# Nine pairs of inner tiles as block products in each feed-forward half of a two-layer decoder trunk

## The chip, the cores and the metric

The kernel runs on one core of a Trainium2 chip. The core has a matrix engine (PE, with its weight loads as PEld), three engines for elementwise work (DVE, ACT and POOL, which is GpSimd) and a queue engine (SP) that mostly issues transfers. The metric is device time in microseconds for the whole program, lower is better. The median of three runs before the change is 2664.32 us (2662.54 to 2666.8).

## The reference

Two layers. Each one is a feed-forward half, a mixer (four kinds of attention with gates), and a second feed-forward half, all on a residual x of 512 tokens by 1024 channels in float32. Only the feed-forward halves change:

```python
def swiglu(h, w_i, w_o):
    gate, up = jnp.split(h @ w_i, 2, axis=-1)
    return (jax.nn.silu(gate) * up) @ w_o

for l in range(DEPTH):                                     # DEPTH = 2
    x = x + 0.5 * swiglu(rms_norm(x, ffn1_norm[l]), ffn1_w_in[l], ffn1_w_out[l])
    ...                                                    # the mixer
    x = x + 0.5 * swiglu(rms_norm(x, ffn2_norm[l]), ffn2_w_in[l], ffn2_w_out[l])
```

`w_i` is 1024 x 5632 and `w_o` is 2816 x 1024, so the inner width of 2816 is 22 tiles of 128.

## The kernel before

All activations stand transposed: channels on the 128 partitions, 512 tokens along the free axis. A product in float32 is made of three matmuls in the type float32r: weight and activation are each split into a high and a low part, and high x high, high x low and low x high are summed (`mm3`, lines 247 to 252). A split is a copy on ACT (high) and a subtraction on DVE (low): `load_split` (line 146) for weights from memory, `split_up` (line 268) for what is already on the core.

A feed-forward half (`ffn`) has two parts. In the inner half, each of the 22 inner tiles takes 16 chained steps over the 8 channel tiles, for gate and for up (`hidden_tile`), 48 matmuls of 512 columns. In the output half, the loop over q takes the 8 output tiles in 4 output pairs (`Pair`), and each sums over the 22 inner tiles.

The inner tiles are of two kinds. The first `nplain = 22 - 2 * npair` are plain: each gives one product of 128 x 128 weights by 512 tokens for each of the two outputs. The others come in pairs, and a pair of inner tiles with a pair of outputs and two halves of 256 tokens makes a 2 x 2 block product in 7 products in place of 8 (Strassen's scheme in Winograd's form). The products have the names a, s, t, b, u, v and d; s, t, u and v use sums of weight tiles: s1 = c + d, s2 = s1 + a, s3 = a + c, s4 = s2 + b. The activation sides (r0 to r3 in `combined`) are made once per half, split, and kept in `fph` and `fpl`, 7 x 256 columns each per pair. Before the change there are 8 pairs, so 6 plain tiles.

`Pair.run` (line 281) does the plain tiles (`whole`), then the pairs in groups of up to four (`group`, line 306). A group loads four weight tiles a, c, d and b, one after another, each with up to 512 columns, one 128 for each pair of the group. Then each of the seven products is split and multiplied over all pairs of the group, so one product of a group of four is 12 matmuls of 256 columns. The buffers matter here: `hi` and `lo`, where splits land, have 4 each and are used in turn by the products in the order a, s, t, b, u, v, d; `raw`, for a and c, has 3; `wb` and `wd`, for b and d, have 1 each; the sums `ws` have 2. A buffer is written again when its last reader is done. The tile d is read first (s1) and last (product d) in its group.

When a product has its last pair, `after` (line 368) folds it into the residual tiles in `y` and `up`, and after v and d the finished tile is stored and the next norm takes its square and its split (`Norm.add`). The square of a tile goes to a tile of the tag `sq`.

The order of the instructions on each engine is made by the framework's planner when the program is built; weight loads, sums and splits of a group have a raised priority (`tc.high_priority`). Each engine then runs its own queue in that order and waits on semaphores. SP issues the weight loads, POOL the residual loads and stores, with descriptors in a ring whose size is `RING`.

Of the kernel before, what the change touches and what calls it, by code (L numbers as in the profile page):

```python
# [12 lines left out]
F32 = mybir.dt.float32  # L13
# [7 lines left out]
P = 128  # L21
# [24 lines left out]
AH = 4  # L46
CW = 512
COL = 64
NPAIRS = (8, 8)
OP_BUFS = dict(x=2, ws=2)  # L50
INTO = dict(b=(0, 0), v=(0, 1), d=(1, 0))
PAD = 24
TH = S // 2
SLOT = dict(a=0, s=5, t=4, b=2, u=1, v=3, d=6)
RING = 8192
OFF = dict(aq=0, ak=512, av=1024, bq=1536, bk=1920, bv=2304, cq=2688, ck=3072, cv=3456,
           dq=3846, dk=4230, dv=4614, gl=4998)
BR_ROW = (0, 512, 896, 1280)
# [41 lines left out]
def trunk_kernel(ctx: ExitStack, tc: tile.TileContext, a, out):  # L100
# [34 lines left out]
    def mm_tile(name):  # L135
        return psm.tile([P, S], F32, tag="mm", name=name)
# [127 lines left out]
    def chain(*args):  # L264
        for _ in chain_steps(*args):
            pass

    def split_up(h, lo, src):
        A.activation(h, src, AF.Copy)
        V.tensor_tensor(lo, src, h.bitcast(F32), ALU.subtract)  # L270

    class Pair:
# [8 lines left out]
        def run(self, out, late=False):  # L281
            self.out = out
            self.x = [self.tile("x", f"x{self.nm}{n}") for n in range(2)]
            for x, src in zip(self.x, self.xs):
                nc.gpsimd.dma_start(x, src)
            n = len(self.paired)
            groups = [(p0, min(4, n - p0)) for p0 in range(0, n, 4)]
            if late:
                assert len(groups) == 1
                self.group(*groups[0], "astu")  # L290
                self.whole()
                self.group(*groups[0], "bvd")
            else:
                self.whole()
                for g in groups:
                    self.group(*g, "astbuvd")
# [95 lines left out]
    def combined(r0, r1, r2, r3):  # L392


        lo, hi = slice(0, TH), slice(TH, S)
        V.tensor_tensor(r2[:, lo], r0[:, lo], r0[:, hi], ALU.subtract)
        V.tensor_tensor(r2[:, hi], r1[:, hi], r2[:, lo], ALU.add)
        V.tensor_tensor(r3, r1[:, lo], r2[:, hi], ALU.subtract)
        V.tensor_tensor(r0[:, hi], r0[:, hi], r1[:, hi], ALU.subtract)


    def ffn(l, w_in, w_out, x_of, nrm, nxt, name, keep, early=None):
        npair = NPAIRS[early is None]
        nplain = NH - 2 * npair
        plain, paired = [], []

        def hidden_tile(j, ip):
            pg = mm_tile(f"pg{name}{j}")
            chain(pg, w_in[l, j, 0], nrm.xh, nrm.xl, f"g{name}{j}")
            pu = mm_tile(f"pu{name}{j}")  # L410
            chain(pu, w_in[l, j, 1], nrm.xh, nrm.xl, f"u{name}{j}")
            g = ip.tile([P, S], F32, tag="g", name=f"g{name}{j}")
            u = ip.tile([P, S], F32, tag="u", name=f"u{name}{j}", bufs=3)
            V.tensor_tensor(g, pg, nrm.rb, ALU.mult)
            A.activation(g, g, AF.Silu)
            V.tensor_tensor(u, pu, nrm.rb, ALU.mult)
            V.tensor_tensor(u, u, g, ALU.mult)
            return u

        with ExitStack() as st:  # L420
            fp = st.enter_context(tc.tile_pool(name=f"ff{name}", bufs=1, reuse_waits="tile"))
            with tc.tile_pool(name=f"fi{name}", bufs=2, reuse_waits="tile") as ip:
                for j in range(nplain):
                    if j == 2 and early is not None:
                        early()
                    u = hidden_tile(j, ip)
                    h = fp.tile([P, S], F32R, tag="fh", name=f"fh{name}{j}", bufs=nplain)
                    lo = fp.tile([P, S], F32R, tag="fl", name=f"fl{name}{j}", bufs=nplain)
                    split_up(h, lo, u)
                    plain.append((h, lo))  # L430
            fq = st.enter_context(tc.tile_pool(name=f"fq{name}", bufs=1, reuse_waits="tile"))
            with tc.tile_pool(name=f"fj{name}", bufs=2, reuse_waits="tile") as ip:
                for p in range(npair):
                    j = nplain + 2 * p
                    r0, r1 = hidden_tile(j, ip), hidden_tile(j + 1, ip)
                    r2 = ip.tile([P, S], F32, tag="r", name=f"r{name}{p}")
                    r3 = ip.tile([P, TH], F32, tag="rs", name=f"rs{name}{p}")
                    combined(r0, r1, r2, r3)
                    h = fq.tile([P, 7 * TH], F32R, tag="fph", name=f"fph{name}{p}", bufs=npair)
                    lw = fq.tile([P, 7 * TH], F32R, tag="fpl", name=f"fpl{name}{p}", bufs=npair)  # L440
                    for n, r in enumerate((r0, r1, r2, r3)):
                        c = slice(n * S, n * S + (S if n < 3 else TH))
                        split_up(h[:, c], lw[:, c], r)
                    paired.append((lambda sl, h=h: h[:, sl], lambda sl, lw=lw: lw[:, sl]))
            nrm.close()
            if nxt is not None:
                nxt.open()
            op = st.enter_context(tc.tile_pool(name=f"fo{name}", bufs=1, reuse_waits="tile"))

            def tile_of(tag, nm):  # L450
                return op.tile([P, TH if tag == "up" else S], F32, tag=tag, name=nm, bufs=OP_BUFS.get(tag, 1))

            for q in range(NK // 2):
                def done(n, x):
                    m = 2 * q + n
                    (nc.sync if nxt is None and m == NK - 1 else nc.gpsimd).dma_start(keep[m], x)
                    if nxt is not None:
                        nxt.add(m, x, lambda nm: tile_of("sq", nm))

                ms = (2 * q, 2 * q + 1)  # L460
                Pair(f"{name}{q}", [w_out[l, m] for m in ms], plain, paired, 0.5, [x_of[m] for m in ms],
                     tile_of).run(done)
# [818 lines left out]
    def kept(name):  # L1281
        return [drm.tile([P, S], F32, name=f"{name}{m}") for m in range(NK)]
# [5 lines left out]
    with tc.tile_pool(name="first", bufs=2) as fp:  # L1288
        x = {}
# [14 lines left out]
    x = [a["x"][m] for m in range(NK)]  # L1304
    for l in range(L):
        xs = kept(f"xs{l}")
        nxt = Norm(l, "nm", f"m_{l}")
        ffn(l, a["f1_in"], a["f1_out"], x, nrm, nxt, f"a{l}", xs, setup_bias if l == 0 else None)
        nxt.finish_cols()
        nrm, nxt = nxt, Norm(l, "n2", f"f2_{l}")  # L1310
        x = kept(f"xt{l}")
        with tc.tile_pool(name=f"acc{l}", bufs=1, reuse_waits="tile") as ap:
            acc = []
            mixer(l, nrm, nxt, xs, x, ap, acc)
        nxt.finish()
        nrm = nxt
        last = l == L - 1
        nxt = None if last else Norm(l + 1, "n1", f"f1_{l + 1}")
        keep = out if last else kept(f"xu{l}")
        ffn(l, a["f2_in"], a["f2_out"], x, nrm, nxt, f"b{l}", keep)  # L1320
        x = keep
        if not last:
            nxt.finish()
            nrm = nxt


def _tiles(w):
    l, k, n = w.shape
    return w.reshape(l, k // P, P, n // P, P).transpose(0, 3, 2, 1, 4).reshape(l, n // P, P, k)


def _out_order(npair):
    first = NH - 2 * npair
    order = list(range(first))
    for p0 in range(0, npair, 4):
        for odd in range(2):
            order += [first + 2 * p + odd for p in range(p0, min(p0 + 4, npair))]
    return order


def _layout(i):
    i = {k: np.asarray(v) for k, v in i.items()}
    r = {"x": i["x"][0].T.reshape(NK, P, S)}
    for n, s in (("f1", "ffn1"), ("f2", "ffn2")):
        t = _tiles(i[s + "_w_in"])
        r[n + "_in"] = np.stack([t[:, :NH], t[:, NH:]], 2)
        t = _tiles(i[s + "_w_out"]).reshape(L, NK, P, NH, P)
        t = np.stack([t[l][:, :, _out_order(NPAIRS[l + (n == "f2") > 0])] for l in range(L)])
        r[n + "_out"] = t.reshape(L, NK, P, HID)
# [42 lines left out]
```

## Time and profile before

| | before |
|---|---|
| median of three runs | 2664.32 us (2662.54 to 2666.8) |
| the profiled execution, its own time | 2664.03 us |
| its span | 2662.2 us |
| PE busy | 2644.1 us, 99% of the span |
| DVE busy | 1735.8 us, 65% |
| ACT busy | 1402.4 us, 53% |
| POOL busy | 349.7 us, 13% |

The span runs from the first to the last instruction of the profiled execution. A matmul's row shows a duration longer than the distance to the next one's start, because matmuls overlap in the engine; so the pace of PE is read from its starts. Names of tiles in the profile leave numbers out: `poa` is `po` of a first feed-forward half (`a`) and `pob` of a second one (`b`). A row such as `hida<-wda` is the high split of product d in a first half, `paa`, `psa` and `pta` are the sums that products a, s and t write.

### The profile page before, as it was taken

Reading aid. Unit: us, or ns where it says so; the run is one execution under the profiler, and the core shown is the slowest. Engines: PE = TensorE matmul, PEld = TensorE weight load, DVE = VectorE, ACT = ScalarE, POOL = GpSimd, SP = SyncE. Lnnn points to the kernel's source line nnn. Section 1 sums busy time; section 2 is a strip of 40 time slices with the busy share of each in tenths; the row PEclk is TensorE's granted clock in tenths of the full one; section 3 lists DMA queues with packets and bytes.
Section 4 is the critical chain, followed back from the end, with each engine's and each line's share of the span. In section 5 each row is a group of like instructions: output and inputs, shape, how many; then the busy total and the mean of one; then the engine's idle time right before and its main releaser. Section 6 shows DMA issues by size and latency. Waiting matters only on the chain.

```text
span 2662.2 us, 40085 instructions
## 1 busy us (share of the span) xinstructions
PE 2644.1 (99%) x14206; PEld 2309.7 (87%) x14206; DVE 1735.8 (65%) x3540; ACT 1402.4 (53%) x2916; POOL 349.7 (13%) x494
## 2 busy tenths in 40 slices
PE   9999999999999999999999999999999999999999
PEld 7888999888988878888988889998889888888898
DVE  5556768777764564557755568587777646645566
ACT  4333458787665643334443334577776556433333
POOL 1000022222222210000000000222222221100000
PEclk9999999999999999999999999999999999999999
DMA  5323442222322343334432334322223223423243
GB/s 167 103 96 103 133 134 73 74 72 89 89 75 80 95 151 101 97 97 122 135 107 95 99 102 141 121 67 79 77 83 94 71 84 100 154 95 97 97 121 118
DMA packets 150985, 272.00 MB, mean 102 GB/s; under 512 B 17977, under 2 KB 48697, under 8 KB 150784
## 3 DMA queue, kind: packets, MB, share of 16 engines
q1 hardware_dynamic: 138960, 233.16, 28.5%
q0 software_dynamic: 10672, 34.19, 4.1%
q8 instruction: 111, 1.82, 0.3%
q10 hardware_dynamic: 1152, 2.10, 0.2%
q14 instruction: 90, 0.74, 0.1%
HBM read 256.70 MB, written 14.90 MB: 102 GB/s over the span
## 4 chain that ended last, share of the span: by engine, by line
PE 96%; DVE 1%; ACT 1%; issue 1%; DMA 1%; POOL 0%; ACTq 0%; POOLq 0%
PE pgl L250 4%; PE pgl L252 4%; PE pgl L251 4%; PE pua L251 3%; PE pua L250 3%; PE pub L252 3%; PE pua L252 3%; PE pub L251 3%; PE pub L250 3%; PE pga L251 3%; PE pga L252 3%; PE pga L250 3%; PE pgb L252 3%; PE pgb L251 3%; PE pgb L250 3%; PE pob L251 2%
## 5 line engine op out<-in xcount | busy, mean ns | idle before, releaser
L250 PE MATMUL pgl<-xhm,higl 128*128 128x512 f32 x512 | 215.7, 421 | 0.0
L252 PE MATMUL pgl<-xhm,logl 128*128 128x512 f32 x512 | 201.0, 393 | 0.0
L251 PE MATMUL pgl<-xlm,higl 128*128 128x512 f32 x512 | 200.5, 392 | 0.0
L250 PE MATMUL pga<-xhf,higa 128*128 128x512 f32 x352 | 137.4, 390 | 2.1 <-ACT xhf L204 2.1
L251 PE MATMUL pga<-xlf,higa 128*128 128x512 f32 x352 | 137.4, 391 | 0.7 <-DVE xlf L205 0.7
L252 PE MATMUL pga<-xhf,loga 128*128 128x512 f32 x352 | 137.7, 391 | 0.0
L250 PE MATMUL pgb<-xhf,higb 128*128 128x512 f32 x352 | 137.7, 391 | 0.0
L252 PE MATMUL pua<-xhf,loua 128*128 128x512 f32 x352 | 137.3, 390 | 0.0
L251 PE MATMUL pua<-xlf,hiua 128*128 128x512 f32 x352 | 137.3, 390 | 0.0
L250 PE MATMUL pua<-xhf,hiua 128*128 128x512 f32 x352 | 137.2, 390 | 0.0
L251 PE MATMUL pub<-xlf,hiub 128*128 128x512 f32 x352 | 136.9, 389 | 0.0
L252 PE MATMUL pub<-xhf,loub 128*128 128x512 f32 x352 | 136.9, 389 | 0.0
L251 PE MATMUL pgb<-xlf,higb 128*128 128x512 f32 x352 | 136.9, 389 | 0.0
L250 PE MATMUL pub<-xhf,hiub 128*128 128x512 f32 x352 | 136.9, 389 | 0.0
L252 PE MATMUL pgb<-xhf,logb 128*128 128x512 f32 x352 | 136.9, 389 | 0.0
L152 ACT ACTIVATE hiua<-rawua 128x512 fp32r<-128x512 f32 x88 | 55.7, 633 | 135.7 <-PE pua L251 119.5
L152 ACT ACTIVATE hiub<-rawub 128x512 fp32r<-128x512 f32 x88 | 55.6, 633 | 131.1 <-PE pub L251 130.4
L155 POOL TENSOR_TENSOR logl<-rawgl,higl 128x512 fp32r<-128x512 f32 x64 | 84.0, 1313 | 249.9 <-ACT higl L152 215.2
L252 PEld LDWEIGHTS pgl<-xhm,logl 128*128 128x128 f32 x512 | 96.1, 188 | 21.9
L155 DVE TENSOR_TENSOR loua<-rawua,hiua 128x512 fp32r<-128x512 f32 x88 | 60.4, 687 | 78.8 <-ACT hiua L152 78.8
L250 PEld LDWEIGHTS pgl<-xhm,higl 128*128 128x128 f32 x512 | 96.6, 189 | 15.8
L251 PEld LDWEIGHTS pgl<-xlm,higl 128*128 128x128 f32 x512 | 96.9, 189 | 13.1
(823 smaller groups left out, 8452.0 us busy)
## 6 DMA issues: line engine op xcount, KB each, us to landing
rawgl<-in_w_gate SPq DMA_DIRECT2D x128, 256.0 KB, 2.6
rawga<-in_f_in SPq DMA_DIRECT2D x88, 256.0 KB, 2.5
rawua<-in_f_in SPq DMA_DIRECT2D x88, 256.0 KB, 2.6
rawgb<-in_f_in SPq DMA_DIRECT2D x88, 256.0 KB, 2.5
rawub<-in_f_in SPq DMA_DIRECT2D x88, 256.0 KB, 2.6
rawmo<-in_w_out SPq DMA_DIRECT2D x32, 256.0 KB, 2.7
rawt0a<-in_w_tok_a SPq DMA_DIRECT2D x32, 192.0 KB, 2.4
rawbqk<-in_w_bqk SPq DMA_DIRECT2D x24, 256.0 KB, 2.6
```

The lines of the kernel that those rows point to most:

```text
L152: A.activation(hi[:, :n], raw[:, :n], AF.Copy)
L155: eng.tensor_tensor(lo[:, :n], raw[:, :n], hi[:, :n].bitcast(F32), ALU.subtract)
L250: T.matmul(ps, wh, xh, start=first, stop=False)
L251: T.matmul(ps, wh, xl, start=False, stop=False)
L252: T.matmul(ps, wl, xh, start=False, stop=last)
```

## The change

Nine pairs in place of eight in each feed-forward half, so 18 inner tiles go through block products and 4 stay plain. The groups have up to three pairs in place of four: three groups of three, with weight tiles of 384 columns and 9 matmuls to a product. The plain tiles of an output are then one weight load of 512 columns in place of two of 512 and 256. Three more edits take memory away: the quarter-size tile `rs` has one buffer in place of two, the squares are written to the tag `y` in place of one of their own, and the descriptor ring is 4096 bytes in place of 8192. `_out_order` lays the weights out on the host in the order in which the groups load them.

```diff
--- before.py
+++ after.py
@@ -46,13 +46,14 @@
 AH = 4
 CW = 512
 COL = 64
-NPAIRS = (8, 8)
+NPAIRS = (9, 9)
+GRP = 3
 OP_BUFS = dict(x=2, ws=2)
 INTO = dict(b=(0, 0), v=(0, 1), d=(1, 0))
 PAD = 24
 TH = S // 2
 SLOT = dict(a=0, s=5, t=4, b=2, u=1, v=3, d=6)
-RING = 8192
+RING = 4096
 OFF = dict(aq=0, ak=512, av=1024, bq=1536, bk=1920, bv=2304, cq=2688, ck=3072, cv=3456,
            dq=3846, dk=4230, dv=4614, gl=4998)
 BR_ROW = (0, 512, 896, 1280)
@@ -284,7 +285,7 @@
             for x, src in zip(self.x, self.xs):
                 nc.gpsimd.dma_start(x, src)
             n = len(self.paired)
-            groups = [(p0, min(4, n - p0)) for p0 in range(0, n, 4)]
+            groups = [(p0, min(GRP, n - p0)) for p0 in range(0, n, GRP)]
             if late:
                 assert len(groups) == 1
                 self.group(*groups[0], "astu")
@@ -434,7 +435,7 @@
                     j = nplain + 2 * p
                     r0, r1 = hidden_tile(j, ip), hidden_tile(j + 1, ip)
                     r2 = ip.tile([P, S], F32, tag="r", name=f"r{name}{p}")
-                    r3 = ip.tile([P, TH], F32, tag="rs", name=f"rs{name}{p}")
+                    r3 = ip.tile([P, TH], F32, tag="rs", name=f"rs{name}{p}", bufs=1)
                     combined(r0, r1, r2, r3)
                     h = fq.tile([P, 7 * TH], F32R, tag="fph", name=f"fph{name}{p}", bufs=npair)
                     lw = fq.tile([P, 7 * TH], F32R, tag="fpl", name=f"fpl{name}{p}", bufs=npair)
@@ -455,7 +456,7 @@
                     m = 2 * q + n
                     (nc.sync if nxt is None and m == NK - 1 else nc.gpsimd).dma_start(keep[m], x)
                     if nxt is not None:
-                        nxt.add(m, x, lambda nm: tile_of("sq", nm))
+                        nxt.add(m, x, lambda nm: tile_of("y", nm))
 
                 ms = (2 * q, 2 * q + 1)
                 Pair(f"{name}{q}", [w_out[l, m] for m in ms], plain, paired, 0.5, [x_of[m] for m in ms],
@@ -1332,9 +1333,9 @@
 def _out_order(npair):
     first = NH - 2 * npair
     order = list(range(first))
-    for p0 in range(0, npair, 4):
+    for p0 in range(0, npair, GRP):
         for odd in range(2):
-            order += [first + 2 * p + odd for p in range(p0, min(p0 + 4, npair))]
+            order += [first + 2 * p + odd for p in range(p0, min(p0 + GRP, npair))]
     return order
```

## Rows read from the trace of the kernel before

**Rows 1.** engine table of the page: busy us, share of the span, instructions

```profile
PE 2644.1 (99%) x14206; PEld 2309.7 (87%) x14206; DVE 1735.8 (65%) x3540; ACT 1402.4 (53%) x2916; POOL 349.7 (13%) x494
```

**Rows 2.** windows view, two groups: PE, PEld, DVE, ACT, POOL busy (instructions), PEclk, DMA, GB/s

```profile
291.00:311.20 20.20, 20.20 (x169) 20.16 (x169) 14.96 (x27) 8.57 (x15) 0.00 (x0) 1.00 0.39 111
```

**Rows 3.** groups by line: engine, tiles, shape, xcount | busy, mean ns | idle before

```profile
L250 PE MATMUL poa<-fha,hioa 128*128 128x512 f32 x96 | 37.4, 390 | 0.0
...
L250 PE MATMUL paa<-fpha,hiaa 128*128 128x256 f32 x64 | 18.1, 282 | 0.0
```

**Rows 4.** timeline of PE: start us, duration us, engine, line, instruction

```profile
254.36 0.39 PE L250 MATMUL poa<-fha,hioa 128*128 128x512 f32 x1
...
262.52 0.28 PE L250 MATMUL paa<-fpha,hiaa 128*128 128x256 f32 x1
...
295.37 0.28 PE L250 MATMUL poa<-fpha,hiba 128*128 128x256 f32 x1
...
302.57 0.28 PE L250 MATMUL psa<-fpha,hisa 128*128 128x256 f32 x1
```

**Rows 5.** timeline of ACT, DVE and SP at one seam, [idle before <-releaser]

```profile
295.50 0.63 ACT L269 ACTIVATE hida<-wda 128x512 fp32r<-128x512 f32 x1 [0.57 <-PE pta L251]
...
296.17 0.69 DVE L270 TENSOR_TENSOR loda<-wda,hida 128x512 fp32r<-128x512 f32 x1 [0.51 <-ACT hida L269]
...
296.89 0.33 SPq L317 DMA_DIRECT2D wda<-in_f_out  x1
...
299.79 0.69 DVE L323 TENSOR_TENSOR s1a<-wca,wda 128x512 f32<-128x512 f32 x1 [1.49 <-DMA wda<-in_f_out]
300.51 0.69 DVE L323 TENSOR_TENSOR s2a<-s1a,waa 128x512 f32<-128x512 f32 x1
...
301.32 0.63 ACT L269 ACTIVATE hisa<-s2a 128x512 fp32r<-128x512 f32 x1 [3.75 <-PE poa L252]
```

**Rows 6.** tile view of wda, then timelines of ACT and PE at three places

```profile
DMA to landing us min/median/max: 2.8/3.0/4.2
...
1681.07 0.63 ACT L269 ACTIVATE hisa<-s2a 128x512 fp32r<-128x512 f32 x1 [5.07 <-PE paa L251]
1681.61 0.62 ACT L269 ACTIVATE hita<-s1a 128x512 fp32r<-128x512 f32 x1
...
1680.88 0.28 PE L252 MATMUL paa<-fpha,loaa 128*128 128x256 f32 x1
1681.76 0.39 PE L250 MATMUL psa<-fpha,hisa 128*128 128x256 f32 x1 [0.60 <-ACT hisa L269]
...
1682.50 0.28 PE L251 MATMUL pta<-fpla,hita 128*128 128x256 f32 x1
...
274.15 0.28 PE L251 MATMUL psa<-fpla,hisa 128*128 128x256 f32 x1
...
274.61 0.28 PE L251 MATMUL pta<-fpla,hita 128*128 128x256 f32 x1
```

**Rows 7.** passes over 384 columns (source, groups), page's DMA issues (KB, us to landing)

```profile
L155 DVE TENSOR_TENSOR lot1a<-rawt1a,hit1a x16: 545/558/1005, 1688.6 to 1759.8; 128x384 fp32r<-128x384 f32 x16
...
L152 ACT ACTIVATE hit1a<-rawt1a 128x384 fp32r<-128x384 f32 x32 | 16.7, 526 | 16.1 <-PE pt1a L544 6.8 <-DMA rawt1a<-in_w_tok_a 4.9 <-issue 1.6
...
rawgl<-in_w_gate SPq DMA_DIRECT2D x128, 256.0 KB, 2.6
...
rawt0a<-in_w_tok_a SPq DMA_DIRECT2D x32, 192.0 KB, 2.4
```

**Rows 8.** timeline of DVE and ACT at the start of the first output half

```profile
260.19 0.69 DVE L323 TENSOR_TENSOR s1a<-wca,wda 128x512 f32<-128x512 f32 x1
...
261.72 0.64 ACT L269 ACTIVATE hisa<-s2a 128x512 fp32r<-128x512 f32 x1 [2.99 <-DVE s2a L323]
```

**Rows 9.** timeline of POOL: DMA issues of the bias table and of its first use

```profile
51.35 0.52 POOL L512 DMA_DIRECT2D scr<-flat  x1 [0.97 <-DMA scr<-flat]
...
373.34 2.15 POOL L529 DMA_DIRECT2D bias0A<-scr  x4
```

## The prediction

> **What bounds the kernel now.** I read the engine table first: PE is busy in 99% of the span [rows 1]. A busy PE need not run at its peak, so the windows view of one stretch of the feed-forward output half comes next. There PE is busy for all of 20.2 us at the full granted clock (1.00, 2.4 GHz), and DVE for 14.96 us, 74% [rows 2]. What the reader is to see there is a PE-bound stage with one engine close behind. The timeline then gives the pitch, the distance between two starts. The 36 matmuls of 512 columns between 254.36 and 262.52 come 0.2267 us apart, the 60 of 256 columns between 295.37 and 302.57 come 0.1200 us apart [rows 4]. The counts by line say how many there are: 96 high-times-high plain matmuls of one layer name are 2 layers x 4 output pairs x 2 outputs x 6 inner tiles, 64 of one block product are 2 x 4 x 8 pairs [rows 3]. So an output pair costs 36 x 0.2267 + 168 x 0.1200 = 28.3 us, and there are 16 of them (4 halves x 4). Last I followed one seam, where group 0 of an output pair ends and group 1 begins, instruction by instruction over four engines [rows 5]. It decides the forecast.
>
> **The matmuls.** For each output pair, two plain inner tiles go: 2 tiles x 2 outputs x 3 = 12 matmuls of 512 columns, 12 x 0.2267 = 2.72 us. One more pair comes: 7 products x 3 = 21 matmuls of 256 columns, 21 x 0.1200 = 2.52 us. The gain is 0.20 us, times 16: 3.2 us. The inner half runs the same matmuls.
>
> The Trainium skill (TensorE: Matmul & The Clock Gate, Back-to-back issue gap) gives a pitch of N/2.4 + 2.5 ns: 215.8 and 109.2 ns, so an estimate of 16 x (2.59 - 2.29) = 4.8 us. The trace does not agree, 226.7 and 120.0 ns [rows 4], and the measurement decides.
>
> **The seam, and why groups of three pairs hurt it.** The sum of weights `s` needs the tile `wd` of its own group (s1 = c + d, s2 = s1 + a), and `wd` has one buffer. So the load of the next `wd` waits until product d of the group before has split its own, and that split waits for a `hi` buffer, which product t releases (four buffers, d comes four after t). From there a chain runs beside PE [rows 5]: hida starts 295.50, loda 296.17, the load is issued 296.89, s1 starts 299.79, s2 300.51, hisa 301.32 and ends 301.95: 6.45 us. PE meanwhile works through b, u, v, d and the next a, 5 x 12 matmuls, and reaches s at 302.57 [rows 4], 7.07 us after hida's start. So the slack is only 0.6 us.
>
> After the change each product has 9 matmuls. PE's cover shrinks by 5 x 3 x 0.1200 = 1.80 us, to 5.27 us. The chain shrinks less. A pass over 384 columns takes 0.558 us on DVE and 0.526 us on ACT [rows 7], against the 0.69 and 0.63 of 512 [rows 5]: -0.13 and -0.10. I take a load of 192 KB as 0.2 us shorter: the page's issue table has 2.4 us for 192 KB and 2.6 for 256 KB [rows 7]. Link by link: 0.57 + 0.59 + 2.70 + 0.59 + 0.68 + 0.53 = 5.66, and 0.06 from hisa's end to the matmul (1681.07 + 0.63 to 1681.76) [rows 6] makes 5.72. So s is 0.45 us late at each seam. There were 16 seams inside output pairs (2 groups each); with 3 groups there are 32. 32 x 0.45 = 14.4 us. The queue of ACT makes it worse: hita stands behind hisa, 0.54 us after it [rows 6], so after two matmuls of s PE may wait some 0.2 us again. I keep that for the range, because PE's order may fill it.
>
> What this looks like can already be seen where a load came late. The load of `wd` takes 3.0 us at the median and 4.2 once; at the seam behind that one PE's starts from 1680.88 to 1682.50 take 1.62 us for 4 steps worth 0.48: 1.14 us lost, with hisa as releaser [rows 6]. One seam per half, the first, also loses 0.22 us (274.15 to 274.61, 2 steps) [rows 6]. 1.14 + 4 x 0.22 = 2.0 us is all that the 16 seams lose now; I take it off, since the 14.4 count every seam anew.
>
> Bounds per seam: below 0, if PE has another product ready. Above: no shorter load (+0.20), the 0.2 behind hita, and t finishing two matmuls later, as it does in groups whose t is interleaved with b (+0.24): 1.1 us, or 35 us in all. I take 0.45, from the row with the usual load.
>
> The Trainium skill (DMA: Bandwidth & Descriptors, Anatomy of one DMA) puts a DMA at about 2.0 us fixed plus bytes/436e3: 2.45 us for 192 KB, 2.60 for 256 KB, so three quarters of the bytes save 0.15 us, which speaks against smaller groups. The trace agrees roughly, 2.4 and 2.6 [rows 7]; by the rule the sum would be 32 x 0.05 = 1.6 us higher.
>
> **The entry of the output half.** PE starts the plain tiles at 254.36 and reaches the first s 12 matmuls of product a after 262.52, at 263.96 [rows 4]. With 24 plain matmuls and 9 of product a it gets there at 254.36 + 5.44 + 1.08 = 260.88. DVE is then still splitting the last pair: s1 starts at 260.19 and hisa ends at 262.35 [rows 8]. With the shorter passes this is 260.06 + 0.59 + 0.68 + 0.53 = 261.86, plus 0.06: 1.04 us late, where there was a slack of 1.55. Four halves: 4.2 us. The bounds are 0 (the last pair's splits can stand behind s1) and 1.4 each. I take 1.04. From one output pair to the next the plain tiles cover: 5.44 + 1.08 us lie between the last d and s, more than the 5.27.
>
> **What costs nothing.** DVE gets 33 passes in place of 22 in an output pair's groups: 11 x 0.558 = 6.1 us of a group's 63 x 0.12 = 7.56, 81%, still under PE; if that cover went, the upper bound above holds it. The small tile of `combined` with one buffer is read within the pair and written again only after two hidden tiles, 96 matmuls or 21.8 us later. The squares wait in `y` for each other and for z: one pass of ACT and one of DVE, 0.63 + 0.69 [rows 5], hidden behind the next plain tiles; at the end of three halves they could show, 3 x 1.3 = 4 us at most, taken as 0. The descriptor ring: GpSimd waits in one place for its own transfers, 0.97 us for the bias table at 51.35, and that table is not read before 373.34 [rows 9]. If half as many fitted, it would wait there for a landing or two more, hidden by over 300 us. In the output half GpSimd has two loads and two stores per 28 us. So 0.
>
> **Sum.** On the profiled execution, 2664.03 us (a span of 2662.2 and 1.8 around it; the median of the three runs is 2664.32, so no correction): 2664.03 - 3.2 + 14.4 + 4.2 - 2.0 = 2677.4 us, 0.5% slower.
>
> **Rivals.**
> - *PE's order covers the seam.* If b or t is split and multiplied ahead of s (t needs only s1, 0.59 us sooner than s2; b needs neither), 0.45 us of lateness is hidden. For it: PE already takes two matmuls of t between those of s [rows 6], and `wb` comes earlier than `wd`. Against: ACT does hisa, then hita, then hiba at each seam that I followed, though hita's operand is ready first, and a later t makes the next d later. Then only the matmuls count: 2664.03 - 3.2 = 2660.8, not slower; down to 2658.8 if the 2.0 us of present stalls go too. It decides from 0.1 us of lateness per seam downwards (32 x 0.1 = the gain of 3.2).
> - *The seam at its upper bound.* Loads as slow as before and t interleaved everywhere: 32 x 1.1 = 35, so 2664.0 - 3.2 + 35 + 4.2 - 2.0 = 2698 us. For it: the load at 1675.31. Against: of the two halves of a pair's groups only one interleaves.
> - *The faster pitch.* Were PE to take 109.2 and 215.8 ns, as the first page's rule says, and the seams covered, it would be 2664.0 - 4.8 - 2.0 = 2657.2. Rows 4 speak against it.
>
> **How the numbers follow.** Forecast 0.50, covered seam 0.34, upper bound 0.09, faster pitch 0.02, and 0.05 for something unseen (0.04 of it no change). 0.2% is 5.3 us, about what a measurement of this kernel tells from no change. The forecast's own range is 2668 to 2692 (0.2 to 0.9 us per seam, entry included), all slower. The covered case lies within 0.2% but for its lowest end, 0.04 of its 0.34. So faster 0.04 + 0.02 + 0.01 = 0.07, same 0.30 + 0.04 = 0.34, slower 0.50 + 0.09 = 0.59. A range from 2659 to 2694 leaves out half of the upper case and the lowest end of the covered one.
>
> **What would show it.** Right: at both seams of an output pair PE's first psa matmul starts 0.3 to 0.7 us after the last paa at pitch, with hisa as releaser, and the chain hida to hisa takes 5.6 to 5.9 us; 12 plain and 21 product matmuls per pair at the same pitches; output halves of 113 + 4 us. Wrong: products b or t ahead of s at the seams and PE at its pitch, output halves near 112.5 us; or a waiting GpSimd.

## The result, and the profile after

The changed kernel takes 2721.18 us (median of 4 runs, 2718.38 to 2723.84), beside 2664.25 us for the kernel before in the same session (4 runs). The ratio is 1.0213, 95% interval 1.0201 to 1.0225: 57 us slower, where 13 were forecast, and above the forecast's range of 2668 to 2692. The profiled span is 2719.8 us, 57.6 more than before.

First the engine table and the chain of waits of the page after (share of the span by engine along the chain that ended last), then the same chain of the page before.

```profile
PE 2665.8 (98%) x14350; PEld 2328.8 (86%) x14350; DVE 1771.4 (65%) x3708; ACT 1419.3 (52%) x3006; POOL 350.7 (13%) x494
...
PE 89%; DVE 4%; DMA 4%; ACT 2%; issue 1%; ACTq 0%; POOL 0%; DVEq 0%; SPq 0%; POOLq 0%
...
PE 96%; DVE 1%; ACT 1%; issue 1%; DMA 1%; POOL 0%; ACTq 0%; POOLq 0%
```

PE still shows 98% of the span [rows 1], so the engine table says almost nothing. The chain says more: before, PE held 96% of it, now 89%, and DMA and DVE have 4% each. The groups by line say that the matmuls are the forecast ones: 64 plain and 72 of one block product, against 96 and 64 [rows 3].

```profile
L251 PE MATMUL poa<-fha,hioa 128*128 128x512 f32 x64 | 25.1, 392 | 0.0
L251 PE MATMUL paa<-fpha,hiaa 128*128 128x256 f32 x72 | 20.3, 282 | 0.0
```

The waits view names the place (who waits, <- for whom: us in total, times, longest). Three rows of after stand first, then one of before.

```profile
DVE s1a L324 <- DMA wda<-in_f_out: 36.2, 18, 4.0
DVE s1b L324 <- DMA wdb<-in_f_out: 34.2, 18, 3.4
PEld psa L251 <- ACT hisa L270: 22.7, 17, 3.1
...
DVE s1a L323 <- DMA wda<-in_f_out: 13.9, 8, 2.8
```

Before, s1 waited 13.9 and 12.1 us for `wd`, 8 times each. Now it waits 36 and 34 us, 18 times each, and PE waits behind it for the split of s, 33 times in all. To size this I took every distance between two starts of PE in the four output halves, less the pitch of its shape [rows 4], and summed what is left. That is 2.4 us before and 60.7 us after. With 3.2 us of matmuls saved, the halves account for 60.7 - 2.4 - 3.2 = 55.1 of the 57.6 us.

The 60.7 us fall into three kinds of place. In all of them s is late: the first matmul of product s starts later than one pitch after the matmul ahead of it, and that excess is the lateness given here. A seam is the step from one group of an output pair to the next, the entry is the first group of an output half.

**The second seam of a pair (group 1 to 2).** A timeline of ACT, DVE, SP and PE at one of them answers to [rows 5]:

```profile
305.01 0.52 ACT L270 ACTIVATE hiva<-wba 128x384 fp32r<-128x384 f32 x1 [1.34 <-DVE wba L324]
305.44 0.51 ACT L270 ACTIVATE hida<-wda 128x384 fp32r<-128x384 f32 x1
...
304.06 0.28 PE L251 MATMUL poa<-fpha,hiba 128*128 128x256 f32 x1
...
305.02 0.28 PE L253 MATMUL pta<-fpha,lota 128*128 128x256 f32 x1
...
306.62 0.33 SPq L318 DMA_DIRECT2D wda<-in_f_out  x1
...
309.11 0.56 DVE L324 TENSOR_TENSOR s1a<-wca,wda 128x384 f32<-128x384 f32 x1 [1.65 <-DMA wda<-in_f_out]
...
310.37 0.52 ACT L270 ACTIVATE hisa<-s2a 128x384 fp32r<-128x384 f32 x1 [3.50 <-DVE s2a L324]
310.80 0.51 ACT L270 ACTIVATE hita<-s1a 128x384 fp32r<-128x384 f32 x1
...
310.18 0.28 PE L253 MATMUL paa<-fpha,loaa 128*128 128x256 f32 x1
310.95 0.38 PE L251 MATMUL psa<-fpha,hisa 128*128 128x256 f32 x1 [0.49 <-ACT hisa L270]
```

From hida's start to the first matmul of s the chain takes 5.51 us, and PE would have reached s at 310.30, 5.28 us after t's last matmul. The chain itself is 0.21 us shorter than forecast (the load takes 2.49 us to s1, not 2.70). But hida starts 0.42 us behind t's last matmul, since it stands behind hiva on ACT, and hiva waits for DVE. 0.42 + 5.51 - 5.28 = 0.65 us late. After two matmuls of s PE loses another 0.28 us in all, as hita stands behind hisa. So 0.93 us at this seam, near the upper bound of 1.1; the median of the fourteen late ones among the sixteen is the same.

The forecast's 0.45 us can be followed to these 0.65. Two matmuls of b now run ahead of t's last one (304.06 and the next), which takes 0.24 us of cover. Hida stands 0.42 us behind t's last matmul, where at the seam of [rows 5] it stood 0.25 behind it (PE, before):

```profile
295.25 0.28 PE L252 MATMUL pta<-fpha,lota 128*128 128x256 f32 x1
```

So 0.45 + 0.24 + 0.17 - 0.21 = 0.65.

**The first seam of a pair (group 0 to 1).** In the first output pair of a half it is like the second or better. In the twelve later ones s is 0.70 to 3.04 us late, 19.7 us together. The worst of them, in a timeline of POOL, SP, DVE and PE:

```profile
1677.52 0.54 POOL L286 DMA_DIRECT2D xa<-xu  x1 [3.45 <-DVE wba L324]
...
1679.17 0.34 SPq L318 DMA_DIRECT2D wda<-in_f_out  x1
...
1683.96 0.56 DVE L324 TENSOR_TENSOR s1a<-wca,wda 128x384 f32<-128x384 f32 x1 [4.03 <-DMA wda<-in_f_out]
...
1682.64 0.28 PE L253 MATMUL paa<-fpha,loaa 128*128 128x256 f32 x1
1685.80 0.58 PE L251 MATMUL psa<-fpha,hisa 128*128 128x256 f32 x1 [2.88 <-ACT hisa L270]
1686.18 0.42 PE L252 MATMUL psa<-fpla,hisa 128*128 128x256 f32 x1
1686.39 0.41 PE L251 MATMUL pta<-fpha,hita 128*128 128x256 f32 x1
```

From the issue of the load to s1 it is 4.79 us here, not 2.49. GpSimd had issued the load of a residual tile 1.65 us earlier. In all twelve such a load is issued 0.5 to 2.3 us ahead of `wd`'s, and there `wd`'s load takes 3.42 us to s1 on the mean (2.73 to 4.79).

What PE does next is seen in the windows view (PE, PEld, DVE, ACT, POOL busy, PEclk, DMA, GB/s):

```profile
1685.80:1691.70 5.90, 5.90 (x27) 5.90 (x28) 3.53 (x7) 2.23 (x5) 0.00 (x0) 0.50 0.43 114
1691.70:1697.00 5.30, 5.30 (x46) 5.30 (x45) 3.36 (x7) 2.30 (x6) 0.00 (x0) 0.97 0.21 46
```

Behind 3.16 us from one start to the next the granted clock is 0.50, the 1.2 GHz level, for 5.9 us. The 256-column matmuls start about 0.21 us apart instead of 0.12. Six such stretches lie in the four output halves, three behind an entry and three behind a seam. They cost 9.6 us beyond the pitch and the 0.28, 2.5 of them in the stretch shown. [Rows 2] of before show 1.00, and its halves have no such stretch.

**The entry.** A row of SP's waits, then a timeline of DVE, SP and PE at the first one; they answer to [rows 8]. The last row is SP's load of `wd` there before:

```profile
SPq L318 <- DVE fpla L271: 17.0, 2, 8.5
```

```profile
257.82 0.68 DVE L271 TENSOR_TENSOR fpla<-ua,fpha 128x512 fp32r<-128x512 f32 x1
...
258.52 0.33 SPq L318 DMA_DIRECT2D wda<-in_f_out  x1
...
260.95 0.56 DVE L324 TENSOR_TENSOR s1a<-wca,wda 128x384 f32<-128x384 f32 x1 [2.11 <-DMA wda<-in_f_out]
...
260.34 0.28 PE L253 MATMUL paa<-fpha,loaa 128*128 128x256 f32 x1
262.79 0.39 PE L251 MATMUL psa<-fpha,hisa 128*128 128x256 f32 x1 [2.17 <-ACT hisa L270]
...
255.99 0.43 SPq L317 DMA_DIRECT2D wda<-in_f_out  x1
```

The first load of `wd` waits up to 8.5 us for a split of the last hidden pair: at the first entry it is issued 0.02 us after DVE has read that pair's tile `u` for the last time (257.82 + 0.68). Before, it was issued at 255.99, ahead of those splits. So s is 2.33 us late here, 9.5 us over the four halves.

In sum: late s at entries 9.5, late s at seams 31.1, the 0.28 us behind each late s 9.2, half clock 9.6, others 1.3.

### The profile page after: what moved, and what is told of

The parts are those of the page before. It is cut to its first block, busy times and chain, and to the rows that moved or that the text cites. A ratio compares the mean times of both kernels' runs of the same rounds, so it can differ in the third digit from the quotient of the medians.

```text
span 2719.8 us, 40867 instructions
## 1 busy us (share of the span) xinstructions
PE 2665.8 (98%) x14350; PEld 2328.8 (86%) x14350; DVE 1771.4 (65%) x3708; ACT 1419.3 (52%) x3006; POOL 350.7 (13%) x494
## 4 chain that ended last, share of the span: by engine, by line
PE 89%; DVE 4%; DMA 4%; ACT 2%; issue 1%; ACTq 0%; POOL 0%; DVEq 0%; SPq 0%; POOLq 0%
PE pgl L251 4%; PE pgl L253 4%; PE pgl L252 4%; PE pua L252 3%; PE pua L251 3%; PE pub L251 3%; PE pub L252 3%; PE pub L253 3%; PE pua L253 3%; PE pga L252 3%; PE pga L253 3%; PE pgb L253 3%; PE pgb L251 3%; PE pgb L252 3%; PE pga L251 3%; DMA wda<-in_f_out 2%
## 5 line engine op out<-in xcount | busy, mean ns | idle before, releaser
L153 ACT ACTIVATE higa<-rawga 128x512 fp32r<-128x512 f32 x88 | 55.5, 632 | 103.4 <-PE pga L252 80.6
```

Source lines behind the costliest of these rows:

```text
L153: A.activation(hi[:, :n], raw[:, :n], AF.Copy)
```

## The experiments

My theory A was: `wd`'s one buffer makes s late at both seams, traffic of the residual tiles makes the first seam worse, the entry waits through shared memory, and the clock falls after the long waits. The rivals were the memory edits (M), and smaller groups or the ninth pair as such (B, N), with their added passes and transfers. All times stand beside runs of the kernel before on the same chip, whose medians were 2664.15 to 2664.83 us. "Gaps" is the sum of PE's start distances over the pitch in the four output halves.

| run | time, us | ratio to before, 95% interval | gaps, us |
|---|---|---|---|
| before | 2664.25 | 1 | 2.4 |
| after | 2721.18 | 1.0213 [1.0201, 1.0225] | 60.7 |
| d_early | 2680.56 | 1.0056 [1.0040, 1.0073] | 15.6 |
| wd2 | 2682.98 | 1.0069 [1.0054, 1.0084] | 17.7 |
| mem_only | 2661.56 | 0.9987 [0.9978, 0.9997] | 2.9 |
| grp3 | 2694.59 | 1.0110 [1.0094, 1.0125] | 27.0 |
| no_resid | 2710.10 | 1.0172 [1.0156, 1.0187] | 48.5 |
| entry | 2706.84 | 1.0164 [1.0150, 1.0178] | 45.4 |
| both | 2667.28 | 1.0011 [1.0002, 1.0020] | 2.1 |
| mix | 2658.81 | 0.9980 [0.9971, 0.9989] | 1.6 |
| exit | 2658.62 | 0.9977 [0.9968, 0.9986] | 2.0 |
| mem_d8 | 2659.88 | 0.9981 [0.9973, 0.9990] | 0.4 |

**d_early: product d right behind t, in groups that are not the last.**

```diff
-                    self.group(*g, "astbuvd")
+                    self.group(*g, "astbuvd" if g is groups[-1] else "astdbuv")
```

> The changed kernel with one edit: in the two groups of an output pair that are not its last, product d is run right behind t instead of last, so that the one buffer of wd is free about 60 matmuls earlier. Theory A (the loop through wd's one buffer, d's split -> load -> s1 -> s2 -> split of s, makes s late at both seams of a pair, and the waits pull the clock down): the 31 us of late s at seams and the 9 us of gaps just behind it go, s stays late at the four entries (9.5 us and some of the half-clock time): 2675 us, 2668 to 2684. Rival B (smaller groups cost by themselves: more splits and more passes on ScalarE and VectorE): nothing moves, 2716 to 2724. Rival C (only a part of the loss hangs on wd; the loads are slow because of the x traffic whatever the order): 2690 to 2705.

Measured 2680.56 us, 40.6 less than after, by one change of order. At the same seam as above, timeline of SP and DVE, then the waits view:

```profile
301.20 0.33 SPq L318 DMA_DIRECT2D wda<-in_f_out  x1
...
303.68 0.56 DVE L324 TENSOR_TENSOR s1a<-wca,wda 128x384 f32<-128x384 f32 x1 [0.17 <-DMA wda<-in_f_out]
```

```profile
PEld psa L251 <- ACT hisa L270: 5.2, 2, 2.8
PEld psb L251 <- ACT hisb L270: 4.9, 2, 2.5
```

The load takes 2.48 us to s1 as before, but it is issued earlier. PE waits for hisa four times in place of 33: the four entries. Smaller groups (B) are still there with all their passes and loads, so these 40.6 us don't come from them. The gaps fall by more than the time, 45.1 us, because PE's two waits for rbm, a tile of the mixer's norm, behind the a halves grow from 3.7 to 6.2 us (see the run "exit").

**wd2: a second buffer for wd, in room gained by narrower tiles.**

```diff
-OP_BUFS = dict(x=2, ws=2)
+OP_BUFS = dict(x=2, ws=2, wd=2)
...
-                return op.tile([P, TH if tag == "up" else S], F32, tag=tag, name=nm, bufs=OP_BUFS.get(tag, 1))
+                w = TH if tag == "up" else GRP * P if tag[0] == "w" else S
+                return op.tile([P, w], F32, tag=tag, name=nm, bufs=OP_BUFS.get(tag, 1))
```

> The changed kernel with the tiles of wb, wd and ws cut to the 384 columns that a group of three uses, and the room given to a second buffer of wd; the order of the products as in the changed kernel. Theory A: with a second buffer the load no longer waits for d's split, so s is in time at the seams, 2665 to 2680, the upper end if the entry still waits for the last pair's split. Rival B (smaller groups by themselves): 2716 to 2724. Rival C (slow loads): 2690 to 2705.

Measured 2682.98 us, 3 us over what I expected. No seam is late any more; s is late at the four entries alone (2.38 to 2.46 us). Two independent ways of freeing `wd` thus give the same time within 3 us. What is left in both beyond the entries is the exit, the step from an a half into its mixer (below), which I had not counted.

**mem_only: the memory edits alone, eight pairs, groups of four.**

```diff
 (before)
-RING = 8192
+RING = 4096
...
-                    r3 = ip.tile([P, TH], F32, tag="rs", name=f"rs{name}{p}")
+                    r3 = ip.tile([P, TH], F32, tag="rs", name=f"rs{name}{p}", bufs=1)
...
-                        nxt.add(m, x, lambda nm: tile_of("sq", nm))
+                        nxt.add(m, x, lambda nm: tile_of("y", nm))
```

> The kernel before with the memory edits alone: rs with one buffer, the squares in y's tile, the descriptor ring at 4 KB; sixteen tiles in pairs and groups of four as before. Theory A: these cost nothing at the seams, 2661 to 2667; if the late first load at the entry comes from the new layout and not from the ninth pair, 4 entries x 2.4 us on top, 2672 to 2676. Rival M (the memory edits make most of the loss): above 2690.

Measured 2661.56 us, 3.3 below before. Rival M falls. The entry is in time here, so its wait comes with the ninth pair's memory, not with these edits. The gain isn't in the output halves (gaps 2.9 against 2.4). The second output half starts at 1220.17 instead of 1222.31, while the first starts within 0.1 us of before, so 2 us of it lie in between. I did not follow that further.

**grp3: groups of three, with eight pairs.**

```diff
 (before)
-            groups = [(p0, min(4, n - p0)) for p0 in range(0, n, 4)]
+            groups = [(p0, min(3, n - p0)) for p0 in range(0, n, 3)]
...
-    for p0 in range(0, npair, 4):
+    for p0 in range(0, npair, 3):
...
-            order += [first + 2 * p + odd for p in range(p0, min(p0 + 4, npair))]
+            order += [first + 2 * p + odd for p in range(p0, min(p0 + 3, npair))]
```

> The kernel before with groups of three pairs (3, 3 and 2) in place of four, nothing else: sixteen tiles, rs with two buffers, squares in their own tile, ring of 8 KB. Theory A: two seams in each of the 32 output pairs, each with a cover about five microseconds long: s late as in the changed kernel, 31 us, with the 9 us behind it and some half-clock time, 2695 to 2715. The forecast's own mechanism at the size that it gave: 32 seams x 0.45 us = 14 us, 2679. Rival M (memory edits) or rival N (the ninth pair itself): 2660 to 2668.

Measured 2694.59 us, 30 over before and just under what I expected. All 32 seams are late, 18.4 us of late s (0.58 each) and 7.3 behind it, and no stretch of the output halves falls to half clock. That is 0.8 us a seam on the mean, but of two kinds: the sixteen between groups of three are 0.72 us late, and the sixteen that lead to a group of two pairs, whose load is shorter, 0.43. So the seam as forecast, without the other troubles, costs about 1.0 us with what lies behind it, twice the 0.45. The gaps account for 24.6 of the 30 us; the rest lies outside the output halves, and I did not follow it. Here the residual load stands farther from `wd`'s. Timeline of POOL, SP and DVE at the first seam of a later pair:

```profile
356.44 0.54 POOL L285 DMA_DIRECT2D xa<-in_x  x1 [2.13 <-DVE xlm L205]
...
360.35 0.33 SPq L317 DMA_DIRECT2D wda<-in_f_out  x1
...
362.82 0.56 DVE L323 TENSOR_TENSOR s1a<-wca,wda 128x384 f32<-128x384 f32 x1 [1.67 <-DMA wda<-in_f_out]
```

It is 3.9 us ahead (3.6 to 4.1 at the nine such seams of the first three halves), and `wd`'s load takes 2.47 us to s1 (mean 2.55). At the three of the last half it is only 2.1 to 2.9 us ahead, and the load still takes no more than 2.54 to 2.65, so the distance alone doesn't tell how slow a load gets. With nine pairs two plain tiles, 2.72 us of matmuls, no longer lie ahead of this seam, so `wd`'s load comes that much sooner after the pair's start, and into the residual's transfer.

**no_resid: residual loads left out.**

```diff
-                nc.gpsimd.dma_start(x, src)
+                nc.gpsimd.memset(x, 0.0)
```

> The changed kernel without the loads of the residual x in the output halves (GpSimd fills the two x tiles with zeros instead, so the residual is left out of the sum); the stores of x stay. Theory A1 (at the first seam of the later output pairs the load of wd is slow, 3 to 4.8 us in place of 2.4, because the store and the loads of x run beside it): these twelve seams, 19.7 us of late s, come down to about the 0.65 us of the second seams, 7.8 us, and most of the half-clock time behind them goes: 2702 us, 2697 to 2708. Rival (the first seam is late by the order of the products or the shorter plain part, not by x): 2716 to 2724.

Measured 2710.10 us, 11.1 less than after, where I expected 13 to 24 less. At the seam where the load took 4.79 us it now takes 2.41 (timeline of SP and DVE):

```profile
1671.65 0.33 SPq L318 DMA_DIRECT2D wda<-in_f_out  x1
...
1674.06 0.56 DVE L324 TENSOR_TENSOR s1a<-wca,wda 128x384 f32<-128x384 f32 x1 [1.73 <-DMA wda<-in_f_out]
```

The twelve first seams go from 19.7 to 10.7 us, their loads from 3.42 to 2.71 us on the mean. So leaving out the residual's loads takes away 9.0 of it. I had expected 7.8 us in place of 10.7: two of the twelve loads still take 3.30 and 3.62 us with no residual load near, and why stays open. Two others are 1.51 and 1.93 us late with a load of 2.46 and 2.56; there the pair's first sum had already waited 1.0 and 1.5 us for `wc`. Three entries and one seam still fall to half clock. So A1's direction stands, and its gain in late s was 9.0 us of the 11.9 that I gave it.

**entry: the first wd tile taken ahead of x.**

```diff
+            self.first = self.tile("wd", f"wd{self.nm}_0") if self.nm[-1] == "0" else None
             self.x = [self.tile("x", f"x{self.nm}{n}") for n in range(2)]
...
-                if n in "bd":
+                if n == "d" and self.first is not None:
+                    r, self.first = self.first, None
+                elif n in "bd":
```

> The changed kernel with one edit of memory: the first pair of an output half takes its wd tile before its x tiles, so that wd lies on other memory than the last hidden tile's u. Theory A2 (the first load of wd waited for the last hidden pair's split, since it lies on that pair's u): s is late by at most 0.5 us at the four entries instead of 2.4: 2710 to 2715 against 2721. Rival (the split of the last pair keeps VectorE busy and delays s1 anyway, or the transfer itself is slow): 2718 to 2723.

Measured 2706.84 us, 14.3 less than after, more than the 6 to 11 that I expected. In the tile view and timelines of DVE and PE:

```profile
L321 SPq DMA_DIRECT2D wda<-in_f_out x1: 425/425/425, 251.5 to 251.5; - x1
```

```profile
259.83 0.55 DVE L327 TENSOR_TENSOR s1a<-wca,wda 128x384 f32<-128x384 f32 x1
...
261.41 0.28 PE L253 MATMUL paa<-fpha,loaa 128*128 128x256 f32 x1
261.67 0.39 PE L251 MATMUL psa<-fpha,hisa 128*128 128x256 f32 x1
```

`wd` is now loaded at 251.5, long before the last pair's splits, and s is 0.13 or 0.14 us late at each of the four entries, not 2.33. The size that I missed is the clock: the three half-clock stretches behind entries, 4.4 us, are gone too. 4 x 2.25 + 4.4 = 13.4.

**both: d_early and entry together.**

```diff
+            self.first = self.tile("wd", f"wd{self.nm}_0") if self.nm[-1] == "0" else None
...
-                    self.group(*g, "astbuvd")
+                    self.group(*g, "astbuvd" if g is groups[-1] else "astdbuv")
...
```

The lines of "entry" that hand this first tile out are in it too.

> The changed kernel with product d early in the groups that are not the last, and the first wd tile taken before x. Theory A: neither seams nor entries are late any more: 2680.6 less 9.9 us of late s at the entries and some 5 us behind them, 2665 us, 2662 to 2670; what is left over the kernel before less 3.2 us (some 6 to 9 us) is the stall at the exit of the two a halves, where a split that waits for its load stands ahead of the norm on ScalarE. Rival (the ninth pair costs elsewhere): 2672 to 2681.

Measured 2667.28 us. Gaps in the output halves are 2.1 us, as few as before. Yet the time is still 2.8 us over before, where 3.2 less of matmuls should show.

**mix: both, with eight pairs in groups of four in the a halves, nine in threes in the b halves.**

```diff
-NPAIRS = (9, 9)
-GRP = 3
+NPAIRS = (8, 9)
+GROUP = {8: 4, 9: 3}
...
-        npair = NPAIRS[early is None]
+        npair = NPAIRS[name[0] == "b"]
...
```

The edits of "both" are in it too, and the lines that take the group's size and the layout of the weights from the new tables.

> As the last one, but eight pairs in groups of four in the a halves (ahead of the mixers) and nine pairs in groups of three in the b halves only. Theory A (the rest of the loss is the exit of the a halves with nine pairs; the memory edits by themselves gave 3 us): 2657 to 2662 us, below the kernel before and at or below the memory edits alone. Rival (the nine pairs cost in the b halves too): 2664 to 2672.

Measured 2658.81 us: 8.5 less, and below the kernel before. So what was left hangs on nine pairs in the a halves, which end before a mixer.

**exit: both, and one split moved on ScalarE.**

```diff
 (both)
...
+            if name[2:] == "a07":
+                with tc.issue_after(norm_act[-1]):
+                    A.activation(hi[:, :n], raw[:, :n], AF.Copy)
+            else:
+                A.activation(hi[:, :n], raw[:, :n], AF.Copy)
```

`norm_act[-1]` is the square root of the mixer's norm (the tile `rcm`); it is recorded where the norm makes it.

> The kernel of the run "both" (nine pairs, d early, the first wd tile ahead of x) with one instruction moved on ScalarE: in the two stages behind the a halves the split of the eighth token-weight tile is put behind the norm's square root instead of ahead of it. Theory A (the rest of the loss is this split, which waits for its load while the norm stands behind it): the two stalls of 2.6 and 3.2 us and the half-clock time behind them go: 2659 us, 2656 to 2662. Rival (the norm at the exit is late for another reason, its own chain on VectorE and ScalarE being as long): 2665 to 2669.

The stall in the run "both" first, timeline of ACT and PE, then a window of the stretch behind it (the columns as above):

```profile
376.09 0.53 ACT L153 ACTIVATE hit0a<-rawt0a 128x384 fp32r<-128x384 f32 x1 [2.35 <-PE pcm L222]
376.64 1.28 ACT L224 ACT_TABLE_LOAD   x1
377.93 0.26 ACT L224 ACTIVATE rcm<-pcm,epsc 128x4 f32<-128x4 f32 x1
...
376.30 0.34 PE L548 MATMUL pt0a<-hit0a,xlm 128*128 128x384 f32 x1
379.19 2.07 PE L234 MATMUL pnm<-rbm,ones 128*128 128x512 f32 x2 [2.55 <-DVE rbm L229]
```

```profile
379.10:382.00 2.90, 2.81 (x5) 1.78 (x6) 0.03 (x1) 0.99 (x2) 0.00 (x0) 0.50 0.24 81
```

The same place in the run "exit", timeline of ACT and PE:

```profile
373.55 1.28 ACT L230 ACT_TABLE_LOAD   x1
375.82 0.26 ACT L230 ACTIVATE rcm<-pcm,epsc 128x4 f32<-128x4 f32 x1 [0.99 <-PE pcm L228]
375.98 0.51 ACT L157 ACTIVATE hit0a<-rawt0a 128x384 fp32r<-128x384 f32 x1
...
377.08 1.12 PE L241 MATMUL pnm<-rbm,ones 128*128 128x512 f32 x2 [0.66 <-DVE rbm L236]
```

Measured 2658.62 us, 8.7 less than the run "both", as expected. The root stands ahead of the split and starts 2.11 us sooner, while pcm, the matmuls whose result it takes, starts 0.21 sooner (374.84 and 375.05). The split's own pass is only 0.53 us of this. In "both" ACT's load of the table for the root, 1.28 us, stands behind the split too; in "exit" it is over before pcm. Before the change seven splits of these weights stand ahead of the root, in the changed kernel eight, in "exit" seven again. PE's wait for rbm falls from 2.55 to 0.66 us, and the half-clock stretch is gone. In "both" the idle time ahead of this split is put down to PE's pcm, on which the split doesn't work. At the second stall of the same run it is put down to the load (ACT):

```profile
1700.60 0.52 ACT L153 ACTIVATE hit1a<-rawt1a 128x384 fp32r<-128x384 f32 x1 [3.04 <-DMA rawt1a<-in_w_tok_a]
```

In d_early the first one shows "DMA rawt0a" as well, 2.51 us, so I read it as a wait for the load there too.

**mem_d8: eight pairs with the memory edits and d early in the first group.**

```diff
 (mem_only)
-                    self.group(*g, "astbuvd")
+                    self.group(*g, "astbuvd" if g is groups[-1] else "astdbuv")
```

> Eight pairs in groups of four as before, with the memory edits and product d early in the first group of a pair. Against the run beside it, this tells what the ninth pair itself is worth with no stall left in either. Theory A (the matmuls alone, 3.2 us less with nine pairs, and a stall or two fewer here): 2659 to 2662, and the run beside it 0 to 3 us below. Rival (nine pairs have a cost of their own on VectorE or in the transfers): the run beside it above this one.

Measured 2659.88 us, beside 2658.62 of nine pairs on the same chip. So with the large stalls gone the ninth pair is worth 1.3 us by the medians. The 3.2 of the matmuls less the difference in gaps, 2.0 - 0.4, would be 1.6. The two intervals overlap, so this is a difference of medians and no more.

## Why the prediction was wrong

- **What bounds the kernel, pitch, matmuls: right.** Counts and pitches are as read. The formula for the pitch that the prediction cites from the Trainium skill (TensorE: Matmul & The Clock Gate, Back-to-back issue gap) is given there for a matmul by itself and not for a stream with weight loads. Only the rival of the faster pitch hangs on it, and the pitch stayed at 226.7 and 120.0 ns. The 3.2 us show only when no stall is left (exit against mem_d8).
- **The seam: the mechanism was right, its size was the step that failed.** "I take 0.45, from the row with the usual load", 32 seams, 14.4 us. Measured over the 32: 31.1 us of late s, 29 x 0.28 = 8.1 behind it, and 5.1 of half clock, 44.3 in all; taking it away gave 45.1 in gaps and 40.6 in time (d_early). Three things were mis-sized.
  - *The terms kept for the upper bound are the usual case.* At the second seams of the changed kernel s is 0.65 us late (median of 14; at the other two, behind the stretches of half clock, it is in time), plus 0.28: hita stands behind hisa and t ends two matmuls later, both as feared, and hida stands behind hiva, which no term had. The shorter load was right and did not make up for it. Groups of three alone give 1.0 (grp3).
  - *"I take a load of 192 KB as 0.2 us shorter" holds only for an undisturbed load.* With two plain tiles fewer the first seam moves 2.72 us nearer to the pair's start, with three pairs ahead of it in place of four another 21 x 0.12 = 2.52, and GpSimd's residual load, which stood 8.2 us ahead of the seam's `wd` before (288.72 to 296.89 in the first half), now stands 0.5 to 2.3 ahead. I had counted those transfers (two loads and two stores per 28 us), but only for GpSimd's own time, not for what they do to SP's. The bound of 1.1 us per seam could not hold 3.04. The fit that the prediction cites from the Trainium skill (DMA: Bandwidth & Descriptors, Anatomy of one DMA) is given there for transfers that GpSimd issues, and these loads are SP's. No term of the sum hangs on it.
  - *The clock was left out.* Three seams fell to 1.2 GHz behind waits of over 2 us. The forecast treated a late s as its lateness alone.
- **The entry: failed by its assumption.** The 4.2 us (1.04 in each of four halves) took `wd` to be in time and DVE's splits of the last pair to set s1. In the changed kernel `wd`'s load waits for such a split: late s 9.5, with the 0.28 and the clock behind it 15.1; taking it away gave 14.3 (entry, from after). With `wd` in time the same edit shows 0.13, not 1.04, since two passes on DVE no longer stand ahead of s1: a's split, which stood among the last pair's splits at 258.44 before, and the split of the second plain load, at 255.17. So even the forecast's own mechanism was too dear there; I had read an edit of memory by what is live in it, not by whose memory a first load comes to lie on.
- **"What costs nothing": mostly right, one place missed.** `rs`, the squares in `y` and the ring cost nothing (mem_only), and with DVE's added passes the output halves still come down to 2.1 us of gaps (both). At the exit I had thought of squares, up to 4 us. What shows instead is one split, and a table load behind it, that the planner puts ahead of the norm's root: PE waits 3.7 us for rbm in the changed kernel (two stalls), and 8.7 us hung on it once the other stalls were gone.
- **The 2.0 us of present stalls** were right (2.4).
- **The rivals.** That PE's order covers the seam fell: t and b are interleaved with s, and no product runs ahead of s. The seam at its upper bound, 2698 us, was nearest, and still 23 short, for the clock, the residual traffic and the entry. That psa starts 0.3 to 0.7 us late with hisa as releaser holds at most of the second seams (0.36 to 0.75, but for two of 1.30 and 1.37 and two in time), and fails at the first ones of the later pairs.

## What to carry to other kernels

A step that shortens the work behind which a single buffer is reloaded moves other queues' transfers against that reload too: list what each queue issues within a few microseconds of it, before and after. Free a single-buffered tile by running its last reader first; here one change of order took back 40.6 of 57 us. Where the forecast has TensorE waiting for over 2 us, price the slower stretch behind the wait as well.

## What the runs showed of the hardware

A load of 192 KB on SP's queue mostly took 2.4 to 2.5 us from its issue to the pass that waits for it when nothing of GpSimd's ran beside it, and up to 4.79 us with a load that GpSimd had issued 1.65 us before. Not all the slow ones have such a neighbour: in the changed kernel's third output half the second seams of the first and the last pair show 3.14 and 3.21 us without one. The Trainium skill (DMA: Bandwidth & Descriptors, Issuing engines are not separate DMA queues) says that transfers started by different engines run on the same 16 DMA engines and interleave. The runs agree as far as they show it: 4.79 us, and 2.41 at the same seam with the GpSimd load left out.

In the changed kernel's output halves PE's granted clock went to 0.50 behind six waits of 2.5 to 3.2 us from start to start, and PE then ran 256-column matmuls about 0.21 us apart for 3.0 to 5.9 us. Not every such wait was followed by it: the first entry of the changed kernel, 2.45 us from start to start, shows none, and the same entry in d_early, 2.50 us, shows 0.50 from 263.8 to 267.0. In no_resid a shorter one, 2.04 us ahead of the seam at 1707.40, was followed by 0.50 from 1708.7 to 1712.1. So the length of the wait doesn't decide it, and no run here tells what does.
